# Rotary embedding on one core: the cos and sin tables come in 16 rows of 4 KB instead of 64 of 1 KB

## The chip, the core and the metric

The kernel runs on one core of a Trainium2 chip. The metric is the device time in microseconds, the median of several executions. A profile of one execution shows the core's engines: TensorE (PE), VectorE (DVE), ScalarE (ACT), GpSimd (POOL), SyncE (SP) and 16 DMA engines that serve the queues of SP, ACT and POOL.

## The reference

`x` is 16 x 512 x 1024 in float32 (33.5 MB), `cos` and `sin` are 512 x 32 (64 KB each), with 16 heads of 64.

```python
x = x.reshape(batch, seq, num_heads, head_dim)
x1, x2 = x[..., :half_dim], x[..., half_dim:]
cos = cos[None, :, None, :]
sin = sin[None, :, None, :]
rotated = np.concatenate([x1 * cos - x2 * sin,
                          x1 * sin + x2 * cos], axis=-1)
```

Each position of the sequence has one row of 32 cosines and 32 sines, which all 16 batches and 16 heads share.

## The kernel before

**Slabs.** Two batches make a slab: 1024 positions of 1024 values, 8 positions to each of the 128 partitions, 32 KB a partition and 4 MB a slab. There are 8 slabs and 5 buffers for them (`slots`). `load(s)` (L60 to L64) issues a slab's load: slabs 0 to 5 from SyncE's queue, 6 and 7 from GpSimd's. Slabs 0 to 4 are loaded at once; slabs 5, 6 and 7 take the buffers of slabs 0, 1 and 2, and their loads are issued when the store of that slab has landed.

**A pass.** A slab is worked on whole, or in two halves for slabs 0, 6 and 7 (L118 to L121). ScalarE casts it to bfloat16 into `xb` (L112). VectorE multiplies by the sine table into `t2`, which lies in the slab's own buffer, and by the cosine table in place (both L133), and adds the two with the halves of each head swapped (L136). ScalarE copies the result back to float32 into the slab (L139) and issues the store from its own queue (L141). The cast of the next pass stands ahead of the work on this one. Each engine works in the order in which its instructions are written by the scheduler; the DMA queue of each issuing engine is worked through in the order of issue.

**The tables.** Partition p holds positions 8p to 8p+7 of a slab of two batches, so partitions 0 to 63 and 64 to 127 need the same 64 rows of tables. `cos` and `sin` are loaded as 64 rows of 256 values (1 KB) into partitions 0 to 63 (L70 to L74), from SyncE's queue, right after the load of slab 0 and ahead of those of slabs 1 to 4. GpSimd builds `pick` (L81 to L88), a matrix of 64 x 128 that copies row r to partitions r and r+64, and the same with a minus sign; it then casts both tables to bfloat16 into `tab1` (L90 to L92). TensorE spreads them with four matmuls into `acc` (L94 to L101): cosine, cosine, minus sine or sine for each half of a head. VectorE copies `acc` to `tab` (L103), which every multiply of L133 reads.

Of the kernel before, what the change touches and what calls it, by code (L numbers as in the profile page):

```python
# [2 lines left out]

# [4 lines left out]


@with_exitstack  # L10
def kernel(
    ctx: ExitStack,
    tc: tile.TileContext,
    x: bass.AP,
    cos: bass.AP,
    sin: bass.AP,
    num_heads: int,
    out: bass.AP,
):
    nc = tc.nc  # L20
    P = nc.NUM_PARTITIONS

    batch, seq, dim = x.shape
    nh = num_heads
    hd = dim // nh
    half = hd // 2
    bf16 = mybir.dt.bfloat16
    f32 = mybir.dt.float32

    nb = 2  # L30
    slots = 5
    nslabs = batch // nb
    rpp = nb * seq // P
    W = rpp * dim
    SP = seq // rpp
    TW = rpp * half

    out_flat = out.rearrange("b s h d -> b s (h d)")

    singles = ctx.enter_context(tc.tile_pool(name="singles", bufs=1))  # L40
    slabs = ctx.enter_context(tc.tile_pool(name="slabs", bufs=slots))
    xpool = ctx.enter_context(tc.tile_pool(name="xpool", bufs=2))
    psum = ctx.enter_context(tc.tile_pool(
        name="psum", bufs=1, space=bass.MemoryType.PSUM))


    def dram(t, s, a=0, n=W):
        return bass.AP(tensor=t.tensor, offset=t.offset + s * nb * seq * dim + a,
                       ap=[[W, P], [1, n]])


    def view(t, offset, *dims):
        return dataclasses.replace(t, offset=t.offset + offset,
                                   ap=[t.ap[0], *[list(d) for d in dims]])


    slab = {}


    def load(s):  # L60

        queue = nc.sync if s < nslabs - 2 else nc.gpsimd
        slab[s] = slabs.tile([P, W], f32, tag="slab", name="slab")
        queue.dma_start(out=slab[s], in_=dram(x, s))  # L64


    load(0)


    cos_sb = singles.tile([SP, TW], f32, tag="cos_sb")  # L70
    sin_sb = singles.tile([SP, TW], f32, tag="sin_sb")
    for t, src in ((cos_sb, cos), (sin_sb, sin)):
        nc.sync.dma_start(out=t, in_=bass.AP(  # L73
            tensor=src.tensor, offset=src.offset, ap=[[TW, SP], [1, TW]]))  # L74

    for s in range(1, slots):
        load(s)

    pick = singles.tile([SP, 2 * P], bf16, tag="pick")  # L81
    nc.gpsimd.memset(pick, 0.0)  # L82
    for g in range(2):
        part = view(pick, g * P, (SP, P // SP), (1, SP))
        nc.gpsimd.affine_select(  # L85
            out=part, in_=part, compare_op=mybir.AluOpType.not_equal,
            fill=1.0 - 2.0 * g, base=0, pattern=[[0, P // SP], [-1, SP]],
            channel_multiplier=1)  # L88

    tab1 = singles.tile([SP, 2 * TW], bf16, tag="tab1")  # L90
    for i, t in enumerate((cos_sb, sin_sb)):
        nc.gpsimd.tensor_copy(out=view(tab1, i * TW, (1, TW)), in_=t)  # L92

    acc = psum.tile([P, 2 * rpp * hd], f32, tag="acc")  # L94
    for i in range(2):
        for h in range(2):
            nc.tensor.matmul(  # L97
                view(acc, i * rpp * hd + h * half, (hd, rpp), (1, half)),
                view(pick, i * h * P, (1, P)),
                view(tab1, i * TW, (half, rpp), (1, half)),  # L100
                start=True, stop=True)  # L101
    tab = singles.tile([P, 2 * rpp * hd], bf16, tag="tab")
    nc.vector.tensor_copy(out=tab, in_=acc)  # L103

    xb = {}


    def cast(u):
        s, r, n = u
        if r == 0:  # L110
            xb[s] = xpool.tile([P, W], bf16, tag="xb", name="xb")
        nc.scalar.copy(out=view(xb[s], r * dim, (1, n * dim)),  # L112
                       in_=view(slab[s], r * dim, (1, n * dim)))

    passes = []  # L118
    for s in range(nslabs):
        n = rpp if 1 <= s < nslabs - 2 else rpp // 2  # L120
        passes += [(s, r, n) for r in range(0, rpp, n)]  # L121


    cast(passes[0])
    for i, (s, r, n) in enumerate(passes):
        if i + 1 < len(passes):
            cast(passes[i + 1])
        xs = view(slab[s], r * dim, (1, n * dim))
        xu = view(xb[s], r * dim, (1, n * dim))

        t2 = view(slab[s].bitcast(bf16), 2 * r * dim, (1, n * dim))
        for t, a in ((t2, rpp * hd), (xu, 0)):
            nc.vector.tensor_mul(  # L133
                out=t, in0=xu,
                in1=view(tab, a + r * hd, (hd, n), (0, nh), (1, hd)))
        nc.vector.tensor_add(  # L136
            out=xu, in0=xu, in1=view(t2, half, (hd, n * nh), (-half, 2), (1, half)))

        nc.scalar.copy(out=xs, in_=xu)  # L139
        if r + n == rpp:  # L140
            nc.scalar.dma_start(out=dram(out_flat, s), in_=slab[s])  # L141
            if s + slots < nslabs:
                load(s + slots)


# [1 line left out]
_INS = ['x', 'cos', 'sin', 'num_heads']  # L147
_OUTS = [((16, 512, 16, 64), 'float32')]

_NUMBERS = {'num_heads': 16}  # L150


# [26 lines left out]
```

## Time and profile before

| | before |
|---|---|
| time, median of 3 runs | 162.8 us (162.47 to 166.78) |
| span of the profiled execution, first to last instruction | 160.2 us |
| ScalarE busy | 113.5 us (71%) |
| VectorE busy | 108.6 us (68%) |
| TensorE busy | 1.0 us, 4 matmuls |
| bytes moved, mean rate | 67.24 MB, 420 GB/s |
| DMA packets | 2464 |
| queue of ACT (stores), of SP, of POOL | 48.5%, 37.5%, 12.1% of 16 engines' span |
| slab 0's first cast begins | 13.38 us |
| first multiply begins | 17.02 us |
| first store issued, last store issued | 37.60 us, 145.54 us |

The page gives no whole time for the profiled execution, only its span; the median of the runs shown is 2.6 us above it. In the profile's lines a number after the engine's name is the source line, "x" the count, and the bracket says how long the engine was idle before and what ended that. Engines in lines with a small q (SPq, ACTq) are the queues that issue DMAs. The page's strips cut the span into 40 slices, with the busy share in tenths.

### The profile page before, as it was taken

The page shows a single profiled execution, that of the slowest core. Times are in us where ns is not written, and L with a number is a line of the kernel's source. Part 1 is how long each engine was busy: PE and PEld are TensorE (multiplying, and loading weights), DVE is VectorE, ACT ScalarE, POOL GpSimd, SP SyncE. Part 2 cuts the span into 40 slices and gives each one's busy share as a digit, 9 for nine tenths or more (in the row PEclk, how much of TensorE's full clock was granted, in tenths as well). Part 3 has the DMA queues.
Part 4 walks back from the last instruction along what each step waited for, and adds up shares of the span by engine and source line. Part 5 has one row for each costly group of instructions (what it writes and reads, how often), then busy time and mean ns, then how long its engine had stood idle before and what let it go on. Part 6 is the DMA issues. An engine that isn't in the chain of part 4 may idle for free.

```text
span 160.2 us, 159 instructions
## 1 busy us (share of the span) xinstructions
PE 1.0 (1%) x4; PEld 0.5 (0%) x4; DVE 108.6 (68%) x34; ACT 113.5 (71%) x23; POOL 3.0 (2%) x11
## 2 busy tenths in 40 slices
PE   0002000000000000000000000000000000000000
PEld 0000000000000000000000000000000000000000
DVE  0001899999979979997997299919839499940000
ACT  3006929998999999899919995089995999553000
POOL 2001000000000000000010001000000000000000
DMA  7999999999999999999999999999999999999995
GB/s 246 409 393 426 393 450 466 393 417 491 401 393 426 491 393 409 499 401 393 483 434 393 450 466 393 426 483 401 409 491 409 393 475 442 393 442 475 393 426 229
DMA packets 2464, 67.24 MB, mean 420 GB/s; under 512 B 288, under 2 KB 416, under 8 KB 416
## 3 DMA queue, kind: packets, MB, share of 16 engines
q10 hardware_dynamic: 1152, 33.55, 48.5%
q1 hardware_dynamic: 1024, 25.30, 37.5%
q0 software_dynamic: 288, 8.39, 12.1%
HBM read 33.69 MB, written 33.55 MB: 420 GB/s over the span
## 4 chain that ended last, share of the span: by engine, by line
DMA 49%; ACT 28%; issue 8%; DVE 4%; SPq 1%; ACTq 0%; POOLq 0%
DMA slab<-in_x_dram 29%; DMA out_dram<-slab 20%; ACT slab L139 16%; ACT xb L112 12%; DVE xb L136 1%; DVE xb L133 1%; DVE slab L133 1%; SPq L73 1%; ACTq L141 0%; SPq L64 0%; POOLq L174 0%; ACTq L139 0%; POOLq L64 0%
## 5 line engine op out<-in xcount | busy, mean ns | idle before, releaser
L112 ACT CAST xb<-slab 128x4096 bf16<-128x4096 f32 (+1 forms) x11 | 56.6, 5155 | 27.8 <-DMA slab<-in_x_dram 26.5
L139 ACT CAST slab<-xb 128x4096 f32<-128x4096 bf16 (+1 forms) x11 | 56.6, 5154 | 3.5 <-DVE xb L136 3.5
L133 DVE TENSOR_TENSOR slab<-xb,tab 128x4096 bf16<-128x4096 bf16 (+1 forms) x11 | 35.9, 3260 | 17.3 <-ACT xb L112 17.2
L133 DVE TENSOR_TENSOR xb<-xb,tab 128x4096 bf16<-128x4096 bf16 (+1 forms) x11 | 35.9, 3261 | 0.3
L136 DVE TENSOR_TENSOR xb<-xb,slab 128x4096 bf16<-128x4096 bf16 (+1 forms) x11 | 35.9, 3261 | 0.3
L103 DVE CAST tab<-acc 128x1024 bf16<-128x1024 f32 x1 | 1.2, 1225 | 15.2 <-PE acc L97 15.2
L64 POOL DMA_DIRECT2D slab<-in_x_dram x2 | 1.2, 608 | 84.1 <-DMA out_dram<-slab 84.1
L112 ACT ACT_TABLE_LOAD x1 | 1.3, 1283 | 0.7 <-PEq L160 0.7
L97 PE MATMUL acc<-tab,pick 64*128 64x256 bf16 x4 | 1.0, 402 | 14.2 <-POOL tab L92 14.2
L92 POOL CAST tab<-cos_sb 64x256 bf16<-64x256 f32 x1 | 0.4, 389 | 12.1 <-DMA cos_sb<-in_cos_dram 12.1
L85 POOL TENSOR_SCALAR_AFFINE_SELECT pick<-pick 64x128 bf16<-64x128 bf16 x2 | 0.5, 285 | 0.1
L97 PEld LDWEIGHTS <-pick 64*128 64x128 bf16 x4 | 0.5, 122 | 14.2 <-issue 12.6
L92 POOL CAST tab<-sin_sb 64x256 bf16<-64x256 f32 x1 | 0.4, 394 | 0.0
L82 POOL MEMSET pick<- 64x256 bf16 x1 | 0.3, 304 | 0.3 <-POOLq L160 0.3
L160 POOL MEMSET const-float32-0.0<- 128x1 f32 x1 | 0.1, 103 | 0.2 <-issue 0.2
L160 POOL MEMSET const-bfloat16-1.0<- 128x1 bf16 x1 | 0.1, 107 | 0.0
L160 POOL MEMSET const-uint8-127<- 128x1 uint8 x1 | 0.1, 106 | 0.0
L160 POOL MEMSET const-float32-1.0<- 128x1 f32 x1 | 0.1, 103 | 0.0
## 6 DMA issues: line engine op xcount, KB each, us to landing
out_dram<-slab ACTq DMA_DIRECT2D x8, 4096.0 KB, 25.9
slab<-in_x_dram SPq DMA_DIRECT2D x6, 4096.0 KB, 26.6
slab<-in_x_dram POOLq DMA_DIRECT2D x2, 4096.0 KB, 24.9
cos_sb<-in_cos_dram SPq DMA_DIRECT2D x1, 64.0 KB, 12.5
sin_sb<-in_sin_dram SPq DMA_DIRECT2D x1, 64.0 KB, 12.3
```

The source lines that it names most:

```text
L64: queue.dma_start(out=slab[s], in_=dram(x, s))
L73: nc.sync.dma_start(out=t, in_=bass.AP(tensor=src.tensor, offset=src.offset, ap=[[TW, SP], [1, TW]]))
L82: nc.gpsimd.memset(pick, 0.0)
L85: nc.gpsimd.affine_select(out=part, in_=part, compare_op=mybir.AluOpType.not_equal, fill=1.0 - 2.0 * g, base=0, pattern=[[0, P // SP], [-1 ...
L92: nc.gpsimd.tensor_copy(out=view(tab1, i * TW, (1, TW)), in_=t)
L97: nc.tensor.matmul(view(acc, i * rpp * hd + h * half, (hd, rpp), (1, half)), view(pick, i * h * P, (1, P)), view(tab1, i * TW, (half, rpp) ...
L103: nc.vector.tensor_copy(out=tab, in_=acc)
L112: nc.scalar.copy(out=view(xb[s], r * dim, (1, n * dim)), in_=view(slab[s], r * dim, (1, n * dim)))
L133: nc.vector.tensor_mul(out=t, in0=xu, in1=view(tab, a + r * hd, (hd, n), (0, nh), (1, hd)))
L136: nc.vector.tensor_add(out=xu, in0=xu, in1=view(t2, half, (hd, n * nh), (-half, 2), (1, half)))
L139: nc.scalar.copy(out=xs, in_=xu)
L160: nc = _bacc.Bacc("TRN2", target_bir_lowering=False, num_devices=1)
```

## The change

Each table is read as 16 rows of 1024 values (4 KB); a row holds four of the old ones, that is 32 positions. They go into one tile `raw` of 128 x 1024 in float32: the cosine's rows to partitions 0, 8, 16, ..., 120 and the sine's to 4, 12, ..., 124. As the other partitions are read too, VectorE clears `raw` first (a memset), and both table loads wait for that. They are still issued from SyncE after slab 0 and ahead of slab 1.

GpSimd's `pick` becomes 128 x 1536: for each of cosine, sine and minus sine four masks of 128 x 128, each of which sends every table row's quarter j to its partitions. They are made with one memset and twelve `affine_select` instead of one and two. One cast of 128 x 1024 to `raw_b` stands in place of two of 64 x 256. TensorE makes each of the four parts of `acc` as a sum of four matmuls, 16 in all instead of 4, each with all 128 rows. From the copy to `tab` on, the source is the same.

```diff
-    load(0)
+    TR = 16
+    TQ = seq // TR // rpp
+    TC = seq * half // TR
+    raw = singles.tile([P, TC], f32, tag="raw")
+    nc.vector.memset(raw, 0.0)
 
-    cos_sb = singles.tile([SP, TW], f32, tag="cos_sb")
-    sin_sb = singles.tile([SP, TW], f32, tag="sin_sb")
-    for t, src in ((cos_sb, cos), (sin_sb, sin)):
-        nc.sync.dma_start(out=t, in_=bass.AP(
-            tensor=src.tensor, offset=src.offset, ap=[[TW, SP], [1, TW]]))
+    def load_tables(queue):
+        for i, src in enumerate((cos, sin)):
+            to = dataclasses.replace(
+                raw, offset=raw.offset + 4 * i * raw.ap[0][0],
+                ap=[[P // TR * raw.ap[0][0], TR], [1, TC]])
+            queue.dma_start(out=to, in_=bass.AP(
+                tensor=src.tensor, offset=src.offset, ap=[[TC, TR], [1, TC]]))
 
+    load(0)
+    load_tables(nc.sync)
     for s in range(1, slots):
         load(s)
 
-    pick = singles.tile([SP, 2 * P], bf16, tag="pick")
+    pick = singles.tile([P, 3 * TQ * P], bf16, tag="pick")
     nc.gpsimd.memset(pick, 0.0)
-    for g in range(2):
-        part = view(pick, g * P, (SP, P // SP), (1, SP))
-        nc.gpsimd.affine_select(
-            out=part, in_=part, compare_op=mybir.AluOpType.not_equal,
-            fill=1.0 - 2.0 * g, base=0, pattern=[[0, P // SP], [-1, SP]],
-            channel_multiplier=1)
+    for g in range(3):
+        for j in range(TQ):
+            part = view(pick, (g * TQ + j) * P + j, (SP, P // SP), (TQ, TR))
+            nc.gpsimd.affine_select(
+                out=part, in_=part, compare_op=mybir.AluOpType.not_equal,
+                fill=-1.0 if g == 2 else 1.0, base=-4 if g else 0,
+                pattern=[[0, P // SP], [-(P // TR), TR]], channel_multiplier=1)
 
-    tab1 = singles.tile([SP, 2 * TW], bf16, tag="tab1")
-    for i, t in enumerate((cos_sb, sin_sb)):
-        nc.gpsimd.tensor_copy(out=view(tab1, i * TW, (1, TW)), in_=t)
+    raw_b = singles.tile([P, TC], bf16, tag="raw_b")
+    nc.gpsimd.tensor_copy(out=raw_b, in_=raw)
 
     acc = psum.tile([P, 2 * rpp * hd], f32, tag="acc")
-    for i in range(2):
-        for h in range(2):
+    for g, at in ((0, 0), (0, half), (1, rpp * hd), (2, rpp * hd + half)):
+        for j in range(TQ):
             nc.tensor.matmul(
-                view(acc, i * rpp * hd + h * half, (hd, rpp), (1, half)),
-                view(pick, i * h * P, (1, P)),
-                view(tab1, i * TW, (half, rpp), (1, half)),
-                start=True, stop=True)
+                view(acc, at, (hd, rpp), (1, half)),
+                view(pick, (g * TQ + j) * P, (1, P)),
+                view(raw_b, j * TW, (half, rpp), (1, half)),
+                start=j == 0, stop=j == TQ - 1)
```

## The prediction

> **What bounds the kernel now.** I read first the strip of the DMA over the span and the queues, then a table of stretches, then the first 17 us in order of time, and last the end of the span.
>
> ```profile
> span 160.2 us, 159 instructions
> PE 1.0 (1%) x4; PEld 0.5 (0%) x4; DVE 108.6 (68%) x34; ACT 113.5 (71%) x23; POOL 3.0 (2%) x11
> DMA  7999999999999999999999999999999999999995
> ...
> DMA packets 2464, 67.24 MB, mean 420 GB/s; under 512 B 288, under 2 KB 416, under 8 KB 416
> ```
>
> Two engines are busy 70% of the time, the DMA engines all of it. The same by stretch (the last two columns are the DMA share and GB/s):
>
> ```profile
> 2.80:13.40 10.60, 0.00 (x0) 0.00 (x0) 0.00 (x0) 0.01 (x1) 0.00 (x0) 1.00 1.00 408
> 13.40:41.00 27.60, 1.01 (x4) 0.39 (x3) 25.05 (x10) 24.11 (x6) 0.73 (x2) 1.00 0.99 423
> 41.00:63.00 22.00, 0.00 (x0) 0.00 (x0) 19.78 (x5) 21.59 (x4) 0.00 (x0) 1.00 1.01 432
> 63.00:85.00 22.00, 0.00 (x0) 0.00 (x0) 20.86 (x6) 18.04 (x4) 0.69 (x1) 1.00 1.02 439
> ...
> 124.20:149.00 24.80, 0.00 (x0) 0.00 (x0) 15.39 (x7) 17.82 (x5) 0.00 (x0) 1.00 1.00 432
> 149.00:160.20 11.20, 0.00 (x0) 0.00 (x0) 0.00 (x0) 0.00 (x0) 0.00 (x0) 1.00 0.82 354
> ```
>
> The packet records agree: between 2.8 and 158 us there are 15 or 16 packets in flight in each sample. A slab is 128 packets of 32 KB, 8 to an engine, mostly 1.213 us each, 9.7 us in all. Sixteen slabs (8 in, 8 out) are 155.3 us; with 2.8 before and 1.3 behind this is 159.4 of the 160.2. So the end moves only if an engine runs dry, or gets more to carry.
>
> Now the part that the change touches:
>
> ```profile
> 1.16 0.52 SPq L73 DMA_DIRECT2D cos_sb<-in_cos_dram  x1
> ...
> 13.38 7.11 ACT L112 CAST xb<-slab 128x4096 bf16<-128x4096 f32 x2 [11.37 <-DMA slab<-in_x_dram]
> 13.75 0.39 POOL L92 CAST tab<-cos_sb 64x256 bf16<-64x256 f32 x1 [12.10 <-DMA cos_sb<-in_cos_dram]
> 14.09 0.39 POOL L92 CAST tab<-sin_sb 64x256 bf16<-64x256 f32 x1
> 14.19 1.01 PE L97 MATMUL acc<-tab,pick 64*128 64x256 bf16 x4 [14.19 <-POOL tab L92]
> ...
> 15.23 1.23 DVE L103 CAST tab<-acc 128x1024 bf16<-128x1024 f32 x1 [15.23 <-PE acc L97]
> 17.02 2.29 DVE L133 TENSOR_TENSOR slab<-xb,tab 128x4096 bf16<-128x4096 bf16 x1 [0.56 <-ACT xb L112]
> ```
>
> The tables land at 13.70 and 13.99, behind slab 0 (13.36). `tab` is ready at 16.46, and the first multiply waits 0.56 longer, for ScalarE's cast. This chain has little slack, but what follows it has. The other place is the end:
>
> ```profile
> 124.22 3.60 ACT L112 CAST xb<-slab 128x4096 bf16<-128x4096 f32 x1 [1.85 <-DMA slab<-in_x_dram]
> ...
> 145.54 0.34 ACTq L141 DMA_DIRECT2D out_dram<-slab  x1
> ```
>
> The last slab lands at 124.20, its store is issued 21.3 us later, and its first packet runs at 148.70, when the store before it leaves an engine. On an idle engine the first load took 1.0 us from its issue to its first packet (0.74 to 1.74), so the last store may be issued up to 147.7: 2.1 us of slack.
>
> **The change, part by part.**
>
> *Transfers.* 128 packets of 1 KB at 46 ns are 8 x 0.046 = 0.37 us on each engine. Now there are 32 of 4 KB, two to an engine if they are dealt evenly: by the slab's rate 1.213/8 = 0.15 each, by four small ones 0.18; 0.30 to 0.37. Gain 0 to 0.07 us; I take 0.05. The landing stays behind slab 0: 13.6 to 14.3, I take 13.95, where the second table lands now. [...]
>
> *The clearing of `raw`.* A new VectorE memset of 128x1024 f32, ahead of both table DMAs; SyncE waits for it. No row shows one; lower bound 0.1 (the constants' memsets on POOL), upper 1.25 (near the 1.23 of the 128x1024 cast). I take 1.25: from 0.74 to 2.0, so the cos table is issued 0.8 us later. Behind it in SyncE's queue stand sin, slabs 1 to 4 and slab 5. Slab 1 was issued at 2.36 and its first packet ran at 12.38: slab 0's transfer hides it all. Without that cover it would cost its 0.8.
>
> *`pick`.* The memset grows from 256 to 1536 columns (0.30 to between 0.30 and 1.8), two selects become twelve of 32 columns (0.10 to 0.285 each, 1.2 to 3.4). POOL is done between 2.5 and 6.5 us, against tables at 13.95: the wait for the tables hides it. Without that cover it would be up to 5 us.
>
> *The cast on POOL.* Two of 256 columns (0.39 each, the first begun before sin is there) become one of 1024, which waits for both. Between 0.39 and 4 x 0.39 = 1.57; from the 128x1 memset (0.10) and this cast (0.39) a column is 1.12 ns, so 1.25, my value. Behind it on POOL stand the loads of slabs 6 and 7, at 79.9 and later.
>
> *Matmuls.* Four start 0.17 to 0.21 us apart, 1.01 in all. Sixteen: 12 x 0.214 more = 3.6. Lower bound 2.2 (12 more at the 0.10 of a weight load, the shortest row on this engine), upper 16 x 0.41 = 6.6 (each waits for the one before, as they now add up in one place). I take 3.6.
>
> *Sum.* 13.95 + 0.05 + 1.25 + 0.05 + 3.6 + 0.05 + 1.23 = 20.2: the first multiply starts there and not at 17.02, 3.2 us later. With the low ends 17.6 (0.6 later), with the high ends 23.9 (6.9 later).
>
> *Where these 3.2 us go.* In the built order VectorE now does both halves' first products, both second ones, then both sums; the first half's sum is fifth of six and not fourth. It ended at 26.05; now five steps of 2.25 from 20.2 give 31.4. ScalarE copies that half back at 30.46 now, when the cast of slab 1 is done; it slips to 31.4, and the first store from 37.6 to 38.6: only 1.0 is left. VectorE's slab 1 ends at 47.2 and not 43.9, ScalarE's copy of it goes from 44.95 to 47.2, and stores 1 to 3 are issued some 2.2 us later: 54.2, 68.6, 82.9. But the store queue is behind: store 1's first packet ran at 60.4, store 2's at 79.7, store 3's at 98.2. Before slab 5, ScalarE waits 3.54 us for its load (84.21); the 2.2 end there.
>
> The 1.0 us of store 0: its first packet ran at 41.0, while loads 3 and 4 were queued until 63.2. Without it they run at full rate 1.0 longer and end 1.0 sooner; no engine is idle. Store 0 then lands at about 62.1 and not 61.1, load 5 begins near 66.2 and not 65.2; while the load queue is empty (62.2 to 66.2) store 1 runs alone, 4.0 x 1/9.7 of it, and ends about 76 and not 77.8, so load 6 is issued 1.7 sooner. Load 5, which then shares with two others, can land 1 to 4 later. Load 6 ends near 103.6 (103.3), load 7 near 123.0 (122.6), and the last store is issued near 146: inside the 2.1 of slack. For 6.9 late the first store slips 4.7; the same steps bring the last one to 146.4. So the terms at the end are 0 and -0.05: span 160.2, and with the 2.6 us that separate it from the shown median, 162.8.
>
> **Rivals.**
>
> *The delay reaches the end (slower).* One mechanism: the late first store shifts the recycled buffers, so the last load lands late, the last store comes after the queue ran dry. For it: the late-issue gaps between a landing and the next load's first packet are uneven (4.1 us for load 5, 5.3 for load 6), and my shares are rough. Against: full engines all the way, 3.54 us of wait at slab 5. It costs nothing up to 2.1 us at the last load, then one for one, and passes 2% from 5.4. With the whole 6.9: 162.8 + 4.8 = 167.6. The plain 3.2 gives 163.9.
>
> *The descriptors are not dealt evenly (slower).* All 32 on one engine: 32 x 0.15 - 0.37 = 4.5 us more on that engine, and since all are full to the end, 167.3; on two engines 164.8. For it: sixteen rows are few, and the trace names no engine for a packet. Against: slabs of 128 rows come out level, the last landings lying within 0.54 us. [...]
>
> *The fewer, larger packets gain (faster).* The most that can go is the difference to the floor of 159.4 and the tables' 0.37: 0.8 + 0.37 us, 161.6, which is within 2%. More would need fewer bytes or a shorter 1.213, and neither changes.
>
> *The change does not do what it says:* rows cut into 1 KB again. Then the transfers are those of now, and the rest, and 162.8, stands.
>
> **Chances.** Forecast and the two cases next to it (no gain, cut rows) 0.74; delay at the end beyond 2% 0.14; uneven dealing 0.08; 0.04 is left for faster, for which I see no mechanism. Two per cent is about what a measurement of this kernel can tell from no change. The range, 161.4 to 166.6, takes the small gain below and most of the way to the slower cases above; the forecast's own is 162.1 to 163.9.
>
> **What would show it.** The first multiply near 20.2 (17.6 to 23.9), a POOL cast of 1.25, sixteen matmuls in 3.6, store 0 issued near 38.6, ScalarE's wait at slab 5 still there, a DMA strip full to the last slice, the last store issued before 147.7. Wrong it would be if the strip showed a dip, if the last landings lay microseconds apart, or if the last load landed after 126.3.

## The result, and the profile after

| | before | after |
|---|---|---|
| median of 6 runs each | 164.79 us (162.47 to 167.10) | 166.54 us (166.25 to 167.05) |
| span of the profiled execution | 160.2 us | 164.7 us |
| first multiply | 17.02 us | 19.71 us |
| slab 1 landed, store 0 issued | 23.52, 37.60 us | 23.09, 38.05 us |
| slab 5 landed | 84.18 us | 94.83 us |
| slab 7 landed, last store issued | 124.20, 145.54 us | 129.11, 150.68 us |

The changed kernel is slower: the ratio is 1.0256 (1.0235 to 1.0276). Three of the six runs before took 162.5 to 162.8 us and three 166.8 to 167.1; all six of the changed kernel took 166.25 us or more. Executions above 165 us occur with the kernel before throughout this study (21 of its 65 runs), and the ratios leave them out. None of them was profiled; the one profile of such a run in which store 0 leaves as early as before (transfers alone, below) looks like the changed kernel's.

The first lines of the page after, with the DMA strip (tenths of 16 engines busy in 40 slices):

```profile
span 164.7 us, 204 instructions
...
DMA  7899999899899999999999999999999999995991
```

There is now a dip in the fourth-last slice. The same stretch, from the table of stretches (the last two columns are DMA share and GB/s):

```profile
124.20:148.00 23.80, 0.00 (x0) 0.00 (x0) 20.63 (x9) 20.19 (x7) 0.00 (x0) 0.50 1.01 435
148.00:152.00 4.00, 0.00 (x0) 0.00 (x0) 0.00 (x0) 2.65 (x1) 0.00 (x0) 0.50 0.57 246
152.00:160.00 8.00, 0.00 (x0) 0.00 (x0) 0.00 (x0) 0.00 (x0) 0.00 (x0) 0.50 0.94 406
```

Up to 148 us the DMA engines are full, as before; then they are idle for two fifths of 4 us. The start, in order of time:

```profile
13.69 1.04 POOL L102 CAST raw_b<-raw 128x1024 bf16<-128x1024 f32 x1 [9.42 <-DMA raw<-in_sin_dram]
14.78 3.57 PE L107 MATMUL acc<-raw_b,pick 128*128 128x256 bf16 x16 [14.78 <-POOL raw_b L102]
...
18.39 1.23 DVE L113 CAST tab<-acc 128x1024 bf16<-128x1024 f32 x1 [16.46 <-PE acc L107]
19.71 4.49 DVE L143 TENSOR_TENSOR slab<-xb,tab 128x4096 bf16<-128x4096 bf16 x2
...
30.90 7.11 ACT L149 CAST slab<-xb 128x4096 f32<-128x4096 bf16 x2 [0.77 <-DVE xb L146]
...
38.05 0.37 ACTq L151 DMA_DIRECT2D out_dram<-slab  x1
```

VectorE does both halves' products side by side ("x2"), so the first half's sum is late: ScalarE waits 0.77 us for it, and store 0 leaves 14.96 us after slab 1 landed. It was 14.08. Before, ScalarE did not wait there (no bracket), and its wait for slab 5 was short:

```profile
30.46 7.11 ACT L139 CAST slab<-xb 128x4096 f32<-128x4096 bf16 x2
37.60 0.38 ACTq L141 DMA_DIRECT2D out_dram<-slab  x1
...
84.21 7.02 ACT L112 CAST xb<-slab 128x8192 bf16<-128x8192 f32 x1 [3.54 <-DMA slab<-in_x_dram]
```

After, slab 5 is the place where 10 us are lost; the lines show it with the end:

```profile
94.85 7.02 ACT L122 CAST xb<-slab 128x8192 bf16<-128x8192 f32 x1 [12.83 <-DMA slab<-in_x_dram]
...
147.04 3.60 ACT L149 CAST slab<-xb 128x4096 f32<-128x4096 bf16 x1 [3.56 <-DVE xb L146]
150.68 0.34 ACTq L151 DMA_DIRECT2D out_dram<-slab  x1
```

ScalarE waits 12.8 us for slab 5, where it waited 3.54. From that cast on, the work of slabs 5, 6 and 7 follows without a wait for a load, 55.8 us to the last store's issue.

The engines' own order shows what happened in between. The records do not name the engine of a packet, but a busy engine's next packet starts within 10 ns of the end of its last one (2158 of the 2160 packets of slabs and tables that follow the first 16 in the kernel before, 2044 of 2064 in the changed one), so each packet can be put to the engine whose last one ended just before it. That gives 16 rows; here three kinds of them, from the fourth slab's end on (r a load's packet of SyncE's queue, W a store's, p a load's of POOL's; the 31 load packets that all begin with are left out):

```
before, 8 of 16 engines  rWWrWrWrWrWrWrrWWWrWrWrWrWrWrrWrWWpWpWpWp...  end 158.4 to 158.8
after, 11 of 16 engines  rWWrWrWrWrWrWrrWWWWW...                       end 161.3 to 161.4
after, 5 of 16 engines   rrWrWrWrWrWrWrWrW...                          end 162.7 to 163.5
```

In the changed kernel eleven engines take store 0's first two packets one after the other. Five take a load more ahead of the first, and a load between the two, and from there on are out of turn with the eleven. On these five the store packets between 51 and 61 us take 1.27 to 1.85 us and those at 67 to 70 us up to 2.48, instead of 1.213. From 31 us on each of the five loses 4.5 to 5.3 us in long packets, each of the other eleven 0.4 to 1.1; before, no engine lost more than 0.6. A slab counts as landed when its slowest engine is done: store 0's landings are spread over 3.6 us (60.55 to 64.19; before 59.64 to 61.12), slab 5's over 7.3 (87.55 to 94.83, and its cast begins at 94.85; before 83.83 to 84.18). So load 5 is issued 3 us later (64.28, behind store 0's last landing at 64.19) and lands 10.7 later.

At the end both groups lose. The eleven run dry for 2.2 to 3.0 us, from 149 to 151.5, because the last store comes too late; the five never run dry, but they are behind and end last.

### The profile page after: what moved, and what is told of

Same layout as the page of the kernel before. It is cut to its first block, busy times and chain, and to the rows that moved or that the text cites. A ratio compares the mean times of both kernels' runs of the same rounds, so it can differ in the third digit from the quotient of the medians.

```text
span 164.7 us, 204 instructions
## 1 busy us (share of the span) xinstructions
PE 3.6 (2%) x16; PEld 2.3 (1%) x16; DVE 109.0 (66%) x35; ACT 113.7 (69%) x23; POOL 5.9 (4%) x20
## 4 chain that ended last, share of the span: by engine, by line
DMA 41%; ACT 23%; DVE 20%; issue 3%; PE 2%; POOL 1%; SPq 0%; ACTq 0%; POOLq 0%; DVEq 0%
DMA slab<-in_x_dram 19%; DMA out_dram<-slab 16%; ACT slab L149 14%; ACT xb L122 9%; DVE slab L143 7%; DVE xb L143 7%; DMA raw<-in_sin_dram 7%; DVE xb L146 5%; PE acc L107 2%; DVE tab L113 1%; POOL raw_b L102 1%; DVE raw L72 1%; SPq L80 0%; ACTq L149 0%; POOLq L102 0%
## 5 line engine op out<-in xcount | busy, mean ns | idle before, releaser
L107 PE MATMUL acc<-raw_b,pick 128*128 128x256 bf16 x16 | 3.6, 418 | 14.8 <-POOL raw_b L102 14.8
L107 PEld LDWEIGHTS <-pick 128*128 128x128 bf16 x16 | 2.3, 145 | 15.5 <-issue 12.2
L96 POOL TENSOR_SCALAR_AFFINE_SELECT pick<-pick 128x32 bf16<-128x32 bf16 x12 | 2.1, 249 | 0.1
L72 DVE MEMSET raw<- 128x1024 f32 x1 | 0.9, 912 | 1.0 <-PEq L170 1.0
L92 POOL MEMSET pick<- 128x1536 bf16 x1 | 1.4, 1378 | 0.3 <-POOLq L170 0.3
L102 POOL CAST raw_b<-raw 128x1024 bf16<-128x1024 f32 x1 | 1.0, 1037 | 9.4 <-DMA raw<-in_sin_dram 9.4
```

Source lines behind the costliest of these rows:

```text
L72: nc.vector.memset(raw, 0.0)
L96: nc.gpsimd.affine_select(out=part, in_=part, compare_op=mybir.AluOpType.not_equal, fill=-1.0 if g == 2 else 1.0, base=-4 if g else 0, pat ...
L102: nc.gpsimd.tensor_copy(out=raw_b, in_=raw)
L107: nc.tensor.matmul(view(acc, at, (hd, rpp), (1, half)), view(pick, (g * TQ + j) * P, (1, P)), view(raw_b, j * TW, (half, rpp), (1, half)), ...
```

## The experiments

The theories: S, the time of store 0 against the load packets decides whether the 16 engines stay in step, that is, each carries its packet of a transfer at about the same time; C, any late compute in the first slabs; T, the transfers of the tables; D, the dry stretch at the end alone; L, lateness itself (it comes in with 32 matmuls). "Store 0 leaves 14.09 us after slab 1" is short for the time from slab 1's landing to the issue of store 0.

**The last store in halves** (the changed kernel)

```diff
-        if r + n == rpp:
+        if s == nslabs - 1:
+            nc.scalar.dma_start(out=dram(out_flat, s, r * dim, n * dim), in_=xs)
+        elif r + n == rpp:
```

> The changed kernel, with the store of the last slab issued in two halves, each as soon as its pass is done (the first some 7 us earlier than the whole one). Theory D (the whole loss is the stretch from 148 to 152 us in which some DMA engines have nothing to do, because the last store is issued at 150.7): the first half fills the gap, no dip is left in the strip, and the time falls by 3 to 4.5 us to 162.0 to 163.5. Rival (the engines lose their time earlier, by falling out of step): no more than 1 us is gained, 165.5 to 166.5.

Measured: 167.07 us median (165.42 to 167.41), ratio 1.027 (1.020 to 1.034). The dip went, the time did not:

```profile
148.00:152.00 4.00, 0.00 (x0) 0.00 (x0) 0.00 (x0) 2.09 (x1) 0.00 (x0) 1.00 0.92 393
```

The first half was issued at 146.51, 4.2 us ahead of the changed kernel's whole store and not 7. Twelve engines now end at 158.5 to 159.2 us, as early as before, but four at 163.5 to 164.2, without a gap. Theory D falls: a single store's end is that of its slowest engine, and those had lost their time by 82 us. It fits the rival, which expected no gain, though the median lies above its 165.5 to 166.5.

**Matmuls alone** (the kernel before with 16 matmuls)

```diff
-        for h in range(2):
+        for h in [0] * 4 + [1] * 4:
```

> The kernel before, with each of the four spreading matmuls done four times, 16 in all; table transfers, masks and casts as before. The tables are ready 2.6 us later and the first multiply starts near 19; VectorE's order is that of before, so store 0 should still be issued near 37.6 and stores 1 to 3 about 1.5 us later. Theory C (any late compute in the first slabs sets off the slow pattern): 166 to 167. Theory S (only the time of store 0 against the load queue decides): store 0 has not moved, 162.3 to 163. Theory T (the table transfers or the later issue of the loads behind them decide): 162.3 to 163.

Measured: 162.07 us (161.91 to 166.12), ratio 0.9988 (0.9970 to 1.0007). The first multiply starts at 19.47, only 0.24 earlier than in the changed kernel, and store 1 is issued at 53.36 and not 51.99:

```profile
19.47 2.29 DVE L133 TENSOR_TENSOR slab<-xb,tab 128x4096 bf16<-128x4096 bf16 x1
...
37.96 0.38 ACTq L141 DMA_DIRECT2D out_dram<-slab  x1
```

Slab 1 landed at 23.87, so store 0 leaves 14.09 us after it, as before. Late tables and later stores alone cost nothing (eight of ten runs below 162.9): C falls.

**Transfers alone** (the changed kernel with 4 matmuls)

```diff
-        for j in range(TQ):
+        for j in range(1):
...
-                start=j == 0, stop=j == TQ - 1)
+                start=j == 0, stop=j == 0)
```

> The changed kernel with 4 matmuls in place of 16: of each sum of four only the first term is made, so three quarters of the table rows are left out of the output's values; transfers, clearing, masks and the cast are the changed kernel's. The first multiply should start near 17.1. Theory T: 166 to 167. Theories C and S: 162.3 to 163, since store 0 is issued near 37.2 and the later stores as before.

Measured: 162.20 us (161.93 to 167.17), ratio 0.9994 (0.9979 to 1.0009): the new transfers, the clearing, the masks and VectorE's new order alone cost nothing (eight of ten runs below 162.6); T falls. The profiled execution was one of the two long ones (span 165.4), and it shows the picture of the changed kernel although store 0 left 14.09 us after slab 1:

```profile
94.30 7.02 ACT L122 CAST xb<-slab 128x8192 bf16<-128x8192 f32 x1 [13.37 <-DMA slab<-in_x_dram]
```

So 14.09 us does not keep the disturbance away; it makes it rarer: two of these ten runs, against all six of the changed kernel.

**24 matmuls** (the kernel before; VectorE's order comes out as in the changed kernel)

```diff
-        for h in range(2):
+        for h in [0] * 6 + [1] * 6:
```

> The kernel before with each spreading matmul done six times, 24 in all. The tables are ready 4.3 us later, VectorE does the two halves of slab 0 side by side as in the changed kernel, and store 0 is issued near 39.2, 1.6 us later than before; transfers as before. Theories C and S: 166 to 167.5. Theory T: 162.3 to 163.

Measured: 164.33 us (164.21 to 164.71), ratio 1.0125 (1.0105 to 1.0144): slower, but by half of what S and C expected, a miss for both. Store 0 leaves 15.65 us after slab 1. Fifteen engines begin rr and one rrr, so all take it later together; twelve of them lose 0.3 to 0.9 us in long packets, four 2.1 to 2.9; slab 5 is cast at 93.08. So an engine can lose time though it takes store 0 in the same turn as all others.

**VectorE's order restored** (the changed kernel, one ordering edge)

```diff
+        if (s, r) == (0, rpp // 2):
+            tc.add_manual_dep(
+                first[0, rpp // 2, True].ins, first[0, 0, False].ins.name,
+                mybir.DependencyInfo(mybir.DependencyClass.NoSync, mybir.DependencyReason.DATA),
+                reason="order")
```

(`first` keeps the two products of each pass.)

> The changed kernel with one thing undone: VectorE's first six operations of slab 0 in the order of before (the first half's sum fourth and not fifth), forced by an ordering edge. Transfers, masks, cast and 16 matmuls stay. The sum of the first half then ends near 28.7, before ScalarE is free, and store 0 is issued 14.1 us after slab 1 lands, as before, not 15.0. Theory S (the time of store 0 against the load packets decides whether the 16 DMA engines stay in step): 162.0 to 163 in most runs. Theory C (tables and later stores late by 2.7 us are enough) and theory T (the transfers of the tables): 166 to 167.

Measured: 162.05 us (161.85 to 167.26, nine of ten below 162.6), ratio 0.9994 (0.9979 to 1.0009). The whole loss is gone with tables that are as late as ever:

```profile
19.78 2.29 DVE L144 TENSOR_TENSOR slab<-xb,tab 128x4096 bf16<-128x4096 bf16 x1
...
30.11 7.11 ACT L155 CAST slab<-xb 128x4096 f32<-128x4096 bf16 x2
...
37.25 0.37 ACTq L157 DMA_DIRECT2D out_dram<-slab  x1
...
86.37 7.02 ACT L122 CAST xb<-slab 128x8192 bf16<-128x8192 f32 x1 [4.04 <-DMA slab<-in_x_dram]
```

ScalarE's copy back no longer waits for VectorE (no bracket), store 0 leaves 14.09 us after slab 1 (23.16), and slab 5 comes 8.5 us earlier than in the changed kernel. The TensorE clock, 0.50 in the changed kernel's stretches above and 1.00 in the kernel before's, is not the cause: three of these ten runs had a mean clock of 0.57 and took 161.85 to 162.02 us, and the changed kernel's one run at 1.0 took 167.05.

**Late by order** (the kernel before, its transfers untouched, 20 matmuls and the changed kernel's order of VectorE)

```diff
-        for h in range(2):
+        for h in [0] * 5 + [1] * 5:
...
+        if (s, r) == (0, rpp // 2):
+            tc.add_manual_dep(
+                first[0, 0, False].ins, first[0, rpp // 2, True].ins.name,
+                ...
+            tc.add_manual_dep(
+                add.ins, first[0, rpp // 2, False].ins.name,
+                ...
```

> The kernel before, its transfers, masks and casts untouched, with 20 matmuls (each five times) and VectorE's first six operations in the changed kernel's order. Store 0 is then issued 14.8 us after slab 1 lands, within 0.2 of the changed kernel. Theory S: 165.5 to 167. Theory T: 162.0 to 163.

Measured: 166.28 us median; three of four runs between 165.98 and 167.01, one at 161.82. With store 0 14.80 us after slab 1, the kernel before takes what the changed kernel takes:

```profile
31.29 7.11 ACT L149 CAST slab<-xb 128x4096 f32<-128x4096 bf16 x2 [0.62 <-DVE xb L146]
...
93.12 7.02 ACT L112 CAST xb<-slab 128x8192 bf16<-128x8192 f32 x1 [10.72 <-DMA slab<-in_x_dram]
```

In this profile two engines of 16 are out of turn; they lose 3.9 and 4.6 us in long packets, 3.1 and 4.1 of it in store packets between 50 and 72 us, and end at 162.6 and 162.9, the other fourteen at 159.7 to 159.8 after a gap of some 1.1 us near 150. Two engines set the time of the kernel. One undisturbed run in four says that 14.8 us makes the disturbance likely, not certain.

**32 matmuls**

```diff
-        for h in range(2):
+        for h in [0] * 8 + [1] * 8:
```

> The kernel before with each matmul done eight times, 32 in all; store 0 is issued about 17.3 us after slab 1 lands, 3.2 later than before, 1.7 later than with 24 matmuls. If lateness itself is what costs (theory L): more than with 24 matmuls, 166 to 168. If the place within a load packet of 1.21 us decides (theory S): 162.3 to 165, no more than with 24.

Measured: 163.27 us (163.09 to 163.42), ratio 1.0066 (1.0047 to 1.0085). Store 0 leaves 17.25 us after slab 1, 2.3 us later than in the changed kernel, and the kernel is 3 us faster than it. Lateness is not what costs; slab 5 is cast at 90.46.

**One queue** (the changed kernel with all slabs in SyncE's queue)

```diff
-        queue = nc.sync if s < nslabs - 2 else nc.gpsimd
+        queue = nc.sync
...
-            nc.scalar.dma_start(out=dram(out_flat, s), in_=slab[s])
-            if s + slots < nslabs:
-                load(s + slots)
+            nc.sync.dma_start(out=dram(out_flat, s), in_=slab[s])
+            if 0 < s <= nslabs - slots:
+                load(s - 1 + slots)
```

> The changed kernel with all slab loads and stores in SyncE's queue, in the order load 0 to 4, store 0, store 1, load 5, store 2, load 6, store 3, load 7, store 4 to 7, so that a DMA engine never has a load and a store to choose between. VectorE's order and store 0's late issue stay. If the loss is that engines take loads and stores in turn out of step (theory S): no engine is behind, the end is near 159.5, 162 to 163 in every run. If it is not: 166 or more; the rival is that a queue that waits for landings runs dry, which costs 1 to 4 us for each dry stretch.

Measured: 177.80 us, ratio 1.096. This is a miss of its own kind. Up to 140 us all engines are within 1 us of each other; then the strip empties, since the scheduler had moved ScalarE's casts of slabs 5 to 7 behind the copies back of the slabs ahead of them, and slabs 6 and 7 were worked on one after the other.

**One queue, ScalarE's order held** (the same, and an edge from each cast to the copy back that it stands ahead of)

```diff
-        nc.scalar.copy(out=xs, in_=xu)
+        back = nc.scalar.copy(out=xs, in_=xu)
+        if i + 1 < len(passes):
+            tc.add_manual_dep(
+                back.ins, ahead.ins.name,
+                ...
```

> As the kernel with one queue, but with ScalarE's order held as in the changed kernel: the cast of the next pass stands ahead of the copy back of this one. In the run with one queue the 16 engines stayed within 1 us of each other up to 140 us, and the queue ran dry only behind that, since ScalarE's order had changed and slabs 6 and 7 were worked on one after the other without overlap. Theory S: with the order held the queue stays full to the end, and although store 0 is issued late (about 15 us after slab 1 lands) every run takes 162 to 163. Rival (a single queue in which loads wait for landings runs dry by itself): 165 or more, with a dip near a load's wait.

Measured: 162.48 us (162.09 to 164.56, 12 runs), ratio 1.0004 (0.9965 to 1.0044). Store 0 is issued 14.9 us after slab 1, as in the changed kernel, and the loss is not there. But the 162 to 163 that theory S expected of every run did not come: four of the 12 took 163.4 to 164.6.

```profile
DMA  7999999999999999999999999999999999999991
...
31.24 7.11 ACT L149 CAST slab<-xb 128x4096 f32<-128x4096 bf16 x2 [0.74 <-DVE xb L146]
...
82.22 7.02 ACT L122 CAST xb<-slab 128x8192 bf16<-128x8192 f32 x1 [0.62 <-DMA slab<-in_x_dram]
```

Here, where no engine can choose between a load and a store, none falls 4 us behind: in this profile, of a run of 163.38 us, the 16 engines' landings of each transfer lie within 1.2 us of each other up to 112 us, and within 1.9 from there to the end. Where that last 1.9 comes from was not followed up.

**The kernel before with one queue** (the last two edits)

> The kernel before with the same single queue and the same held order of ScalarE; tables as before. Theory S: 162.0 to 162.6 in every run, with none near 166. If a single queue gains more (no engine ever chooses between a load and a store), 161.5 to 162. Rival: 165 or more.

Measured: 163.04 us (162.19 to 163.72, 12 runs), ratio 1.0021 (0.9991 to 1.0052). None is near 166, but the undisturbed time is not bettered: the runs scatter over 1.5 us, and the 162.0 to 162.6 that was expected of every run did not come. No version was found that beats the kernel before's undisturbed runs.

All of it in one table, sorted by the one number that theory S names, from each profiled execution:

| kernel | store 0 issued after slab 1 landed | slab 5 cast at | median | runs above 165 us |
|---|---|---|---|---|
| before | 14.08 us | 84.21 us | 164.79 us (of the 6; undisturbed 162.5) | 21 of 65 |
| order restored | 14.09 | 86.37 | 162.05 | 1 of 10 |
| matmuls alone | 14.09 | 87.08 | 162.07 | 2 of 10 |
| transfers alone | 14.09 | 94.30 (long execution) | 162.20 | 2 of 10 |
| late by order | 14.80 | 93.12 | 166.28 | 3 of 4 |
| last store in halves | 14.92 | 94.29 | 167.07 | 4 of 4 |
| changed | 14.96 | 94.85 | 166.54 | 6 of 6 |
| 24 matmuls | 15.65 | 93.08 | 164.33 | 0 of 4 |
| 32 matmuls | 17.25 | 90.46 | 163.27 | 0 of 5 |

The time rises by 4 us between 14.1 and 14.9, and falls again behind it. The three kernels that separate the parts (matmuls, transfers, order) each cost nothing; late tables and the new order together, with or without the new transfers, cost all of it. What is shown is that how often the loss comes goes with the time at which store 0 meets the load queue (runs above 165 us: 26 of 95 at 14.08 and 14.09, 13 of 14 from 14.80 to 14.96, none of 9 at 15.65 and 17.25), and that none of the 24 runs with one queue and ScalarE's order held took more than 164.56 us.

What is not shown is why an engine's packets are stretched, to twice their length at worst. The mix of loads and stores at that moment does not explain it: the longest of the changed kernel, at 67 to 70 us, ran while only 3 to 7 of the other 15 engines carried loads, and in the kernel before 145 store packets ran while six or more of the others did, none over 1.23 us. Nor is it shown what decides, at one and the same 14.1 us, which executions are disturbed.

## Why the prediction was wrong

Right were the parts ahead of store 0. The first multiply was forecast at 20.2 and came at 19.71; the tables landed at 13.36 and 13.54 (forecast 13.95), the cast took 1.04 (1.25), the sixteen matmuls 3.57 (3.6), the memset of `raw` 0.91 (1.25), and POOL was done with `pick` at 4.3. Also the new order of VectorE and its effect were foreseen: store 0 at 38.6, measured 38.05.

The step that failed is "The 1.0 us of store 0", with its "no engine is idle". The working took the 16 DMA engines for one server that shares evenly between queues. It gave store 0's landing as 62.1 (64.19), load 5 landing "1 to 4 later" (10.7), load 7's last packet at 123.0 (127.5), the last store at 146 (150.7). But the rows above show the engines sharing packet by packet, 1.2 us at a time, each for itself. Store 0 came 0.9 us later against slab 1, most of a packet, and five of them took another turn than the rest. The terms of bytes were right. The term for the time that single engines lose was not in the sum at all, and measured 4.5 to 5.3 us on five engines; and eleven engines did go idle, for 2.2 to 3.0 us. Why those packets were long stays open, as said above.

A smaller term was off as well: the 2.6 us added to the span. In the runs that give both, the time is 1.8 us above the span.

The sign that was missed stood in the times shown: one run of three at 166.78, with nothing in the bytes to explain it. This kernel's bytes are the same in every run and it still takes two times, so it has a second way of running; the change made that way the usual one.

The first rival, the delay that reaches the end, named the right place (the recycled buffers, a last load that lands late, a queue that runs dry) and the right threshold: the last store was 3.0 us past the 147.7 that was worked out. But its price, the delay itself, was wrong in kind: 0.9 us at store 0 became 10.7 at slab 5. By its rule the last load, 4.9 us late, would have cost 2.8; the span grew by 4.5. And the dry queue was only a part of it, as the last store in halves showed.

The rival of uneven dealing did not come about: each 4 KB packet took 0.159 us, within the 0.15 to 0.18 of the working, and the 16 engines' landings of a table lie within 0.52 us, which leaves no room for an engine that carries all 32 (32 x 0.159 = 5.1 us). The two tables land 0.18 us apart (13.36 and 13.54), where 0.29 lay between them before. Neither matters for the time: transfers alone took 162.20 us, ratio 0.9994. Behind store 0's first packets the rows above show r and W in turn, in packets of 32 KB that take 1.213 us where nothing disturbs them. The working used the mean of that and not the turns.

The marks that the prediction set for being wrong were the right ones: a dip in the strip, last landings microseconds apart (161.61 to 163.83) and a last load after 126.3 (129.11).

## What to carry to other kernels

With several queues on 16 DMA engines, look at the spread of a transfer's landings and not only at the mean share: here slab 5's landings lay 7.3 us apart (87.55 to 94.83) and its cast began at 94.85, when the slowest engine was done, and in the run "late by order" two engines of 16 cost 4 us while the strip, behind its first slice, read 8 or 9 up to 147 us. Where the runs of a kernel fall into two groups, find out what separates them before pricing an edit by bytes, since here an edit that moved one store by 0.9 us, less than a packet of 1.213, chose the group. And a late input can cost through the scheduler: here the order that it chose for the late tables, not the lateness, moved the store (14.96 us after slab 1 and not 14.09), and one ordering edge undid it (162.05 us and not 166.54).

## What was not expected of the hardware

A store's packet of 32 KB, 1.213 us where nothing disturbs it, took up to 2.48 us on engines that took store 0 out of turn with the others; nothing here says why. Time over lateness was not monotone: store 0 at 14.9 us after slab 1 cost 4 us, at 17.25 only 1.
